# Up projection of a gated MLP: tokens as the stationary operand, gate and up columns side by side, and seven products for a part of it

## The chip, the core and the metric

The kernel runs on one core of a Trainium2 chip. A core has five engines with an instruction queue each: TensorE (PE, matrix products, its weight loads shown as PEld), VectorE (DVE), ScalarE (ACT), GpSimd (POOL) and SyncE (SP). TensorE reads operands from SBUF, the on-chip memory of 128 partitions, and writes to PSUM, which has eight banks of 128 x 512 float32. VectorE and ScalarE read and write both. DMA queues move data between HBM and SBUF; in this kernel SP issues the loads of weights.

The metric is the device time of one execution in microseconds. Before the change the runs shown took 1553.33, 1554.3 and 1554.38 us, median 1554.3.

## The reference

One layer of a decoder trunk over 256 tokens of width 2048: a token mixer (gated delta rule and pooling) with its input and output projections, then a gated MLP with a causal convolution, then a last norm. The change touches the MLP:

```python
        h = rmsnorm(x, norm_ffn_w[l])
        gate, up = jnp.split(jnp.einsum('bsd,df->bsf', h, w_up[l]), 2, axis=-1)
        gate = causal_dwconv(gate, conv_ffn_w[l]) + conv_ffn_b[l]
        x = x + jnp.einsum('bsf,fd->bsd', jax.nn.gelu(gate, approximate=False) * up, w_down[l])
    return rmsnorm(x, norm_final_w)
```

w_up is 2048 x 11264 (5632 columns of gate, then 5632 of up), w_down 5632 x 2048, the convolution reaches over three tokens. All is float32.

## The kernel before

**Products in three passes.** TensorE is given float32 data in a rounded form (F32R). Each operand is split into a high part and the remainder, and a product is the sum of high x high, low x high and high x low. A weight tile is 256 rows by 512 columns, held as 128 partitions x 2 x 512 ("raw", 512 KB). begin() (L198 to L219) loads it by SP, ScalarE casts it to whi (L209), VectorE subtracts to give wlo (L217). weights() (L145) hands out the next tile, in the order of the list srcs, and splits up to AHEAD = 2 tiles further on; whi and wlo have three buffers each, raw has four.

**Up projection (L1192 to L1221).** It goes over 11 pairs of 512 gate columns and 512 up columns; the list srcs (L95) holds for each pair first the eight gate tiles, then the eight up tiles. gemm_b() (L256) makes one of the two: the weight tile is the stationary operand, 128 columns at a time, and the tokens move, high and low part side by side as 512 columns (L272), then the high part alone against wlo as 256 columns (L273). So a tile takes eight couples of matmuls. The result lies in four banks with features on partitions and tokens along the free dimension, and it takes the banks of psm and psg in turn, so that one result can be emptied while the next is made. merged() (L277) adds the two halves of a bank; ScalarE and VectorE then scale by the norm (rb2, a row of factors copied over the partitions, L1165), convolve along tokens with one tensor_scalar and two scalar_tensor_tensor (L1200, L1204), apply Gelu (L1206), multiply by up (L1208) and split the product into hhi and hlo (L1215, L1216), the operands of the down projection.

**Down projection (L1256 on).** Here tokens are the stationary operand, and the 512 columns of a weight tile move. products() (L1244) issues for one tile and 128 tokens two times three matmuls of 512 columns; a plain tile is 12 matmuls. Three of the 11 feature chunks, SEVEN = (4, 9, 10), are made by Strassen's scheme in Winograd's form: a 2 x 2 block product (two halves of the tokens, two of the features, two of the columns) by seven products instead of eight, with sums of activations made by half_sums() (L1175) and sums of weights T1 to T4 made by VectorE in the buffer of the loaded block ("quad", quarter() at L161, the subtraction at L204). A product is six matmuls and has its own split weights. Between the products stand plain tiles.

**Turning.** turned() (L285) transposes a 256 x 512 block on TensorE, 16 transposes of 128 x 128 in two banks; before the change the mixer alone calls it (L293).

**Order.** From the output projection on, the order of the instructions on each engine's queue comes from a planner, which takes among those that it believes ready the one that stands first in the program; issue_after() puts the instructions of a block behind a given one on its engine. On the chip each queue runs strictly in that order.

**Names in the changed code.** xt holds the residual; fhl the normed tokens, high and low, features on partitions, in four tiles of 512 features (fhl[0] is features 0 to 511); rs2 is the norm's factor for each token. pm() gives two banks of the pool psm (two such buffers), pg() one bank of psg (four).

Of the kernel before, what the change touches and what calls it, by code (L numbers as in the profile page):

```python
# [14 lines left out]
P = 128  # L15
# [20 lines left out]
def kernel(  # L36
# [58 lines left out]
    for c in range(DFF // 512):  # L95
        srcs += cols(w_up[0], 512 * c, KD) + cols(w_up[0], DFF + 512 * c, KD)
    down = [cols(w_down[0], 512 * c, KF) for c in range(4)]

    SEVEN = (4, 9, 10)
# [59 lines left out]
    quarters = {}  # L159

    def quarter(half, chunk, what):  # L161

        if what == "11":
# [34 lines left out]
    def begin(n):  # L198
        while len(made) < min(len(srcs), n):
            load(len(made) + 1)  # L200
            raw = loads[len(made)]
            if isinstance(raw, tuple):
                raw, plus, minus = raw
                nc.vector.tensor_tensor(raw, plus, minus, op=ALU.subtract)  # L204
            shape = list(raw.shape)
# [13 lines left out]
            made.append((hi, lo))  # L219

# [912 lines left out]
    xt = fp.tile([P, 2, D], F32, name="xt")  # L1133
# [5 lines left out]
    for c in range(4):  # L1139
# [24 lines left out]
    rb2 = cpool.tile([P, S], F32, tag="rb", name="rb2")  # L1164
    rs2 = rstd_rows(ssq2, rb2)  # L1165
# [7 lines left out]
    def half_sums(c):  # L1173

        h = whole[c]  # L1175
        a11, a12, a21, a22 = (h[:, 2 * j : 2 * j + 2, t * P : (t + 1) * P] for t in range(2) for j in range(2))
        s = fp.tile([P, 4, S], F32, tag="y", name=nm("sums"))
# [5 lines left out]
        if c == SEVEN[1]:  # L1183
            hi, lo = (lambda b: (b[:, 0], b[:, 1]))(big.tile([P, 2, 4, S], F32R, tag="x3", name="sx"))
        else:
            more = dict(tag="gs", bufs=2) if c == SEVEN[2] else {}
            hi, lo = (fp.tile([P, 4, S], F32R, name=f"s{n}{c}", **more) for n in ("hi", "lo"))
        nc.scalar.copy(hi, s)
        nc.vector.tensor_tensor(lo, s, hi.bitcast(F32), op=ALU.subtract)
        sums_of[c] = (hi, lo)  # L1190

    rb2b = rb2.unsqueeze(1).to_broadcast([P, 4, S])  # L1192
    for c in range(DFF // 512):
        ps = gemm_b(lambda k: both(fhl, k), KD)
        gs = fp.tile([P, 4, S], F32, tag="gs", bufs=2, name=nm("gs"))
        nc.vector.tensor_tensor(gs, merged(ps, gs), rb2b, op=ALU.mult)
        y = fp.tile([P, 4, S], F32, tag="y", name=nm("y"))
        for f in range(4):
            r = 4 * c + f
            nc.vector.tensor_scalar(y[:, f, :], gs[:, f, :], cfw[:, 2 * KF + r : 2 * KF + r + 1],  # L1200
                                    vec[:, V_CB + r : V_CB + r + 1], op0=ALU.mult, op1=ALU.add)
            for j in (1, 0):
                s = 2 - j
                nc.vector.scalar_tensor_tensor(y[:, f, s:], gs[:, f, : S - s], cfw[:, j * KF + r : j * KF + r + 1],  # L1204
                                               y[:, f, s:], op0=ALU.mult, op1=ALU.add)
        nc.scalar.activation(y, y, AF.Gelu)  # L1206
        ps = gemm_b(lambda k: both(fhl, k), KD)
        nc.vector.tensor_tensor(gs, merged(ps, gs), y, op=ALU.mult)  # L1208
# [6 lines left out]
        nc.scalar.copy(hh, gs)  # L1215
        nc.vector.tensor_tensor(hl, gs, hh.bitcast(F32), op=ALU.subtract)  # L1216
        hhi.append(hh)
        hlo.append(hl)
        whole[c] = gs
        if c == SEVEN[0]:  # L1220
            half_sums(c)  # L1221
# [3 lines left out]
    lh, ll = at(hhi), at(hlo)  # L1225
# [17 lines left out]

    def products(ps, high, low, w, first, last, cs=slice(0, 512), shared=False):  # L1244
        for kk in range(2):
            for n, (part_, lhs) in enumerate(((w[0], high), (w[0], low), (w[1], high))):
                mm(ps[:, cs], lhs(kk), part_[:, kk, cs], start=(first and kk == 0 and n == 0),  # L1247
# [153 lines left out]
```

## Time and profile before

| what | value |
|---|---|
| median of three runs | 1554.3 us |
| profiled execution | 1552.15 us |
| its span, first to last instruction | 1550.4 us |
| granted TensorE clock, mean | 0.998 |
| read from HBM / written | 299.66 MB / 5.28 MB |

The busy time of an engine is a share of the span. A row of a group tells line, engine, operation, what it writes and reads, count, busy time, mean length of one in ns, and the engine's idle time ahead of it with what ended it. Timeline rows begin with the start in us and the length in us; a matmul's record is longer than the spacing between two matmuls, since they overlap. A row of stretches tells for each engine its busy time and, as (x...), how many instructions touch the stretch, then the granted clock, the DMA share and GB/s. Rows of one line of the kernel give minimum, median and maximum in ns, and the first and last start.

### The profile page before, as it was taken

What the parts mean: (1) busy time and instruction counts of PE and PEld (TensorE: products, weight loads), DVE (VectorE), ACT (ScalarE), POOL (GpSimd) and SP (SyncE); (2) the same over time, 40 slices, a digit from 0 to 9 for tenths busy, and PEclk for the clock granted to TensorE, in tenths of its full rate; (3) what the DMA queues carried; (4) which work ended last, traced back from release to release, by engine and by line L of the source; (5) the groups of instructions that cost most, each with busy time, mean ns of one, the idle gap of its engine ahead of it and who ended that gap; (6) DMA issues with size and microseconds to landing.
All of it is one profiled execution on the core that took longest, in us unless ns stands there. A gap on an engine that the chain in (4) does not pass through costs nothing.

```text
span 1550.4 us, 21200 instructions
## 1 busy us (share of the span) xinstructions
PE 1541.6 (99%) x7942; PEld 1294.1 (83%) x7942; DVE 1151.4 (74%) x1749; ACT 770.3 (50%) x987; POOL 39.3 (3%) x54
## 2 busy tenths in 40 slices
PE   9999999999999999999999999999999999999998
PEld 8888888788888888888888888888888888888886
DVE  6788858996689858886656667767666677877885
ACT  6445446454545446454554544444444444555552
POOL 1010001000100000000000000000000000000000
PEclk9999999999999999999999999999999999999999
DMA  8776757776576756675656666666666668557662
GB/s 274 214 219 206 204 152 223 215 209 183 170 237 202 208 164 202 217 206 175 215 181 185 187 186 188 189 190 189 184 195 186 187 189 271 176 190 231 201 209 93
DMA packets 165846, 306.34 MB, mean 198 GB/s; under 512 B 19138, under 2 KB 23010, under 8 KB 165614
## 3 DMA queue, kind: packets, MB, share of 16 engines
q1 hardware_dynamic: 162720, 299.95, 64.2%
q10 hardware_dynamic: 3022, 5.03, 1.0%
q8 instruction: 62, 1.02, 0.3%
q14 instruction: 42, 0.34, 0.1%
HBM read 299.66 MB, written 5.28 MB: 197 GB/s over the span
## 4 chain that ended last, share of the span: by engine, by line
PE 98%; issue 1%; DMA 1%; DVE 0%; ACT 0%; POOL 0%; POOLq 0%; ACTq 0%
PE psm L250 15%; PE psm L248 15%; PE psm L249 15%; PE psm L272 11%; PE psg L272 11%; PE psm L1247 7%; PE psg L1247 7%; PE psg L273 5%; PE psm L273 5%; PE psm L391 1%; PE psg L293 1%; PE psg L781 1%; PE psg L783 0%; DMA vrow<-ev 0%; PE psm L309 0%
## 5 line engine op out<-in xcount | busy, mean ns | idle before, releaser
L209 ACT CAST whi<-raw 128x1024 fp32r<-128x1024 f32 x500 | 526.0, 1052 | 612.9 <-PE psm L249 281.8
L217 DVE TENSOR_TENSOR wlo<-raw,whi 128x1024 fp32r<-128x1024 f32 x498 | 607.3, 1222 | 287.6 <-ACT whi L209 284.5
L250 PE MATMUL psm<-wlo,xhl 128*128 128x512 f32 x864 | 339.7, 393 | 0.6 <-DVE wlo L217 0.6
L248 PE MATMUL psm<-whi,xhl 128*128 128x512 f32 x864 | 338.6, 392 | 0.0
L249 PE MATMUL psm<-whi,xhl 128*128 128x512 f32 x864 | 337.9, 391 | 0.0
L272 PE MATMUL psm<-fhl,whi 128*128 128x512 f32 x704 | 246.1, 396 | 0.0
L272 PE MATMUL psg<-fhl,whi 128*128 128x512 f32 x704 | 238.2, 395 | 0.0
L273 PE MATMUL psm<-fhl,wlo 128*128 128x256 f32 x704 | 194.3, 279 | 0.0
L250 PEld LDWEIGHTS psm<-wlo,xhl 128*128 128x128 f32 x864 | 162.2, 188 | 35.1 <-DVE wlo L217 1.9
L249 PEld LDWEIGHTS psm<-whi,xhl 128*128 128x128 f32 x864 | 162.3, 188 | 33.4
L248 PEld LDWEIGHTS psm<-whi,xhl 128*128 128x128 f32 x864 | 162.3, 188 | 33.3 <-issue 0.2
L273 PE MATMUL psg<-fhl,wlo 128*128 128x256 f32 x704 | 178.9, 280 | 0.0
L272 PEld LDWEIGHTS psm<-fhl,whi 128*128 128x128 f32 x704 | 131.3, 188 | 30.4
L272 PEld LDWEIGHTS psg<-fhl,whi 128*128 128x128 f32 x704 | 129.2, 188 | 24.3
L273 PEld LDWEIGHTS psg<-fhl,wlo 128*128 128x128 f32 x704 | 132.5, 188 | 6.9
L273 PEld LDWEIGHTS psm<-fhl,wlo 128*128 128x128 f32 x704 | 132.6, 188 | 1.2
L209 ACT CAST whi<-quad 128x1024 fp32r<-128x1024 f32 x42 | 44.3, 1054 | 47.5 <-PE psm L1247 27.6
L217 DVE TENSOR_TENSOR wlo<-quad,whi 128x1024 fp32r<-128x1024 f32 x42 | 51.3, 1222 | 18.0 <-ACT whi L209 17.3
L1247 PE MATMUL psm<-whi,hhi 128*128 128x512 f32 (+1 forms) x150 | 58.0, 387 | 0.0
L1247 PE MATMUL psm<-whi,hlo 128*128 128x512 f32 (+1 forms) x150 | 58.0, 386 | 0.0
L1247 PE MATMUL psm<-wlo,hhi 128*128 128x512 f32 (+1 forms) x150 | 57.8, 386 | 0.0
L248 PE MATMUL psm<-whi,mhi 128*128 128x512 f32 x128 | 50.9, 397 | 0.0
(323 smaller groups left out, 1699.4 us busy)
## 6 DMA issues: line engine op xcount, KB each, us to landing
raw<-in_w_in_dram SPq DMA_DIRECT2D x224, 512.0 KB, 4.2
raw<-in_w_up_dram SPq DMA_DIRECT2D x176, 512.0 KB, 4.5
raw<-in_w_down_dram SPq DMA_DIRECT2D x64, 512.0 KB, 4.6
raw<-in_w_out_dram SPq DMA_DIRECT2D x32, 512.0 KB, 3.8
quad<-in_w_down_dram SPq DMA_DIRECT2D x12, 1024.0 KB, 6.2
mv<-vrow SPq DMA_DIRECT2D x12, 512.0 KB, 4.4
taps<-in_conv_qkv_w_dram SPq DMA_DIRECT2D x16, 256.0 KB, 6.5
raw<-in_pool_w_dram SPq DMA_DIRECT2D x8, 512.0 KB, 3.9
```

What stands on the lines that cost most here:

```text
L209: nc.scalar.copy(hi, raw)
L217: last_split[0] = nc.vector.tensor_tensor(lo, raw, hi.bitcast(F32), op=ALU.subtract).ins
L248: mm(ps[:, t, :], lh(k, t), hi[:, kk, :], start=(k == 0), stop=False)
L249: mm(ps[:, t, :], ll(k, t), hi[:, kk, :], start=False, stop=False)
L250: mm(ps[:, t, :], lh(k, t), lo[:, kk, :], start=False, stop=(k == nk - 1))
L272: mm(ps[f], hi[:, kk, fs], rhl(k), start=(k == 0), stop=False, skip_group_check=True)
L273: mm(ps[f][:, 1, :], lo[:, kk, fs], rhl(k)[:, 0, :], start=False, stop=(k == nk - 1), skip_group_check=True)
L293: nc.tensor.transpose(pt[:, ff, t * P : (t + 1) * P], src[:, t, f * P : (f + 1) * P], ident)
L391: mm(ps_k0[:, t, :], part(k, t), w[:, kk, :], start=(k == 0 and w is hi and part is xh), stop=(k == KD - 1 and w is lo))
L781: mm(pg0, kq[:, h, 0, 0:P], kq[:, h, :, :], start=True, stop=True)
L1247: mm(ps[:, cs], lhs(kk), part_[:, kk, cs], start=(first and kk == 0 and n == 0), stop=(last and kk == 1 and n == 2), skip_group_check=shared)
```

## The change

1. The order of the weight tiles in the up projection: gate and up tiles of a pair alternate (gate one ahead). Both results of a pair are made in four banks at once: (column, token half) with column 0 for gate and 1 for up.
2. Tokens are the stationary operand and the weight's 512 columns move, by products(), as in the down projection.
3. For pairs 1 to 10 the first 512 of the 2048 contracted features (FOUR = 0, four of the 16 tiles) are made by seven products. The 2 x 2 block is: token halves, the two halves of these features, and gate and up as the two halves of the columns. Sums of activations are made once (up_sums); sums of weights for each pair in a buffer "quad" of the tag xt. The banks of the pair serve as accumulators: product 11 is copied by ScalarE to another bank, two sums are written by VectorE into the others, and one bank carries the running sum. The seven stand ahead of the pair's 12 whole tiles.
4. The result has tokens on partitions. ScalarE copies it out of PSUM (gate scaled by rs2), TensorE turns it with turned(), in the midst of the next pair's seven products; ScalarE makes the first tap of the convolution, VectorE the two others, from PSUM. The last pair is turned at the head of the down projection.
5. The residual xt is stored to DRAM and loaded again after the up projection, since quad takes its place in SBUF.
6. In the down projection SEVEN becomes (8, 9, 10); the activations of chunks 8 and 9 are put together from their high and low parts before they are summed.

```diff
+    FOUR = 0
+    UP_PARTS = ("T1", "11", "T2", "21", "T3", "22", "T4")
+    up_w = [(cols(w_up[0], 512 * c, KD), cols(w_up[0], DFF + 512 * c, KD)) for c in range(NUP)]
+    up_steps = []
+    for c in range(NUP):
+        kps = [kp for kp in range(KD // 2) if c == 0 or kp // 2 != FOUR]
+        order = [(0, kps[0])]
+        for a, b in zip(kps[1:], kps):
+            order += [(0, a), (1, b)]
+        order.append((1, kps[-1]))
+        if c:
+            srcs += [("up", c, what) for what in UP_PARTS]
+        srcs += [up_w[c][col][kp] for col, kp in order]
+        up_steps.append(order)
...
-    SEVEN = (4, 9, 10)
+    SEVEN = (8, 9, 10)
...
+    UP_BUFFER = {"11": 0, "T1": 1, "T2": 1, "T3": 0, "21": 2, "22": 3, "T4": 1}
+    def quad_load(c, n):
+        if n == 0:
+            t = fp.tile([P, 4, 2, 512], F32, tag="xt", name=nm("quad"))
+            for i in range(4):
+                up_quarters[i] = t[:, i]
+        i = (1, 0, 3, 2)[n]
+        last_load[0] = nc.sync.dma_start(up_quarters[i], up_w[c][i % 2][2 * FOUR + i // 2]).ins
+    def up_sum(what):
+        b11, b12, b21, b22 = (up_quarters[i] for i in range(4))
+        for out_, plus_, minus_ in {"T1": [(b12, b12, b11)], "T2": [(b12, b22, b12)],
+                                    "T3": [(b11, b12, b11), (b12, b12, b21)]}[what]:
+            nc.vector.tensor_tensor(out_, plus_, minus_, op=ALU.subtract)
...
             made.append((hi, lo))
+            if following is not None:
+                up_sum(following)
+            if isinstance(src, tuple) and src[2] == "T4":
+                last_quad_split[0] = last_split[0]
...
+        nc.scalar.dma_start(xt_d[:, :, c * 512 : (c + 1) * 512], xs)
...
-    rs2 = rstd_rows(ssq2, rb2)
+    rs2 = rstd_rows(ssq2, None)
...
+    def gate_part(c, pts):
+        y = fp.tile([P, 4, S], F32, tag="y", name=nm("y"))
+        for f in range(4):
+            r = 4 * c + f
+            pt = pts[f // 2][:, f % 2, :]
+            with tc.issue_after(last_copy[0]) if c < NUP - 1 else ExitStack():
+                nc.scalar.activation(y[:, f, :], pt, AF.Identity, scale=cfw[:, 2 * KF + r : 2 * KF + r + 1],
+                                     bias=vec[:, V_CB + r : V_CB + r + 1])
+            with tc.issue_after(last_quad_split[0]) if c < NUP - 1 else ExitStack():
+                for j in (1, 0):
+                    s = 2 - j
+                    nc.vector.scalar_tensor_tensor(y[:, f, s:], pt[:, : S - s], cfw[:, j * KF + r : j * KF + r + 1],
+                                                   y[:, f, s:], op0=ALU.mult, op1=ALU.add)
+            if f == 1:
+                yield
         nc.scalar.activation(y, y, AF.Gelu)
...
+    def up_part(c, pts):
+        y = whole[c]
+        for f2, pt in enumerate(pts):
+            fs = slice(2 * f2, 2 * f2 + 2)
+            nc.vector.tensor_tensor(y[:, fs], pt, y[:, fs], op=ALU.mult)
...
+    def split_parts(c):
+        ups = up_ups[0]
+        bank = banks_of[c]
+        y = pg()
...
+        chain_ = bank[0, 1]
+        part("T1", y, True)
+        own = cpool.tile([P, 512], F32, tag="sqj", name=nm("own"))
+        nc.scalar.copy(own, y)
+        part("11", chain_, True)
+        last_copy[0] = nc.scalar.copy(bank[0, 0], chain_).ins
+        yield
+        part("T2", chain_, False)
+        nc.vector.tensor_tensor(bank[1, 0], chain_, own, op=ALU.add)
+        part("21", bank[0, 0], False)
+        yield
+        part("T3", chain_, False)
+        nc.vector.tensor_tensor(bank[1, 1], chain_, own, op=ALU.add)
+        part("22", bank[1, 0], False)
+        part("T4", chain_, False)
...
+    for c in range(NUP):
+        pair = [pm(), pm()]
+        banks_of[c] = {(0, 0): pair[0][:, 0], (1, 0): pair[0][:, 1], (1, 1): pair[1][:, 0], (0, 1): pair[1][:, 1]}
+        bank = banks_of[c]
+        if c:
+            parts = split_parts(c)
+            next(parts)
+            gates = gate_part(c - 1, turned(pending[0]))
+            next(parts)
+            ups = turned(pending[1])
+            for _ in parts:
+                pass
+        steps_ = up_steps[c]
+        left = len(steps_)
+        pending = []
+        for n, (col, kp) in enumerate(steps_):
+            left -= 1
+            w = weights()
+            for t in range(2):
+                products(bank[col, t], lambda kk: fh(2 * kp + kk, t), lambda kk: fl(2 * kp + kk, t), w,
+                         c == 0 and kp == 0, not any(q[0] == col for q in steps_[n + 1 :]), shared=True)
+            if c and n < 3:
+                next(gates) if n < 2 else up_part(c - 1, ups)
+            if c + 1 < NUP:
+                if left in (8, 7, 6, 5):
+                    quad_load(c + 1, 8 - left)
+                if left == 4:
+                    up_sum("T1")
+            if not any(q[0] == col for q in steps_[n + 1 :]):
+                e = fp.tile([P, 2, 512], F32, tag=("eg", "eu")[col], name=nm("e"))
+                for t in (0, 1) if col == 0 else (1, 0):
+                    if col == 0:
+                        nc.scalar.activation(e[:, t, :], bank[col, t], AF.Copy, scale=rs2[:, t : t + 1])
+                    else:
+                        nc.scalar.copy(e[:, t, :], bank[col, t])
+                pending.append(e)
+            if c == 0 and n == 8:
+                up_ups.append(up_sums())
+            if c == NUP - 1 and n == 5:
+                half_sums(SEVEN[0])
+    xt = fp.tile([P, 2, D], F32, tag="xt", name="xt")
+    for c in range(4):
+        nc.scalar.dma_start(xt[:, :, c * 512 : (c + 1) * 512], xt_d[:, :, c * 512 : (c + 1) * 512])
...
+            if hf == 0 and n == 1:
+                for _ in gate_part(NUP - 1, turned(pending[0])):
+                    pass
+            if hf == 0 and n == 2:
+                up_part(NUP - 1, turned(pending[1]))
```

In the code a product is named by the weights it takes: 11, 21 and 22 are loaded tiles, T1 to T4 sums of them. eg and eu are the copies of the gate and up banks in SBUF.

More of the change, by code (lines that the diff above doesn't have):

```diff
@@ L204, in begin @@
                 nc.vector.tensor_tensor(raw, plus, minus, op=ALU.subtract)
+            src = srcs[len(made)]
+            following = {"T1": "T2", "T2": "T3"}.get(src[2]) if isinstance(src, tuple) and src[0] == "up" else None
             shape = list(raw.shape)
@@ L1171, with four_sums @@
     sums_of = {}
[L1173 to L1177, printed above, removed]
+    def four_sums(a11, a12, a21, a22, hi, lo):
+        s = fp.tile([P, 4, S], F32, tag="s", name=nm("sums"))
         s1, s2, s3, s4 = (s[:, n].rearrange("p (k s) -> p k s", k=2) for n in range(4))
@@ L1242, in weighted @@
         nc.vector.tensor_tensor(block(t, c), block(t, c), nfin[:, c * 512 : (c + 1) * 512], op=ALU.mult)
[L1244 to L1247, printed above, removed]
-                   stop=(last and kk == 1 and n == 2), skip_group_check=shared)
     def direct(ps, kp, t, w, first, last, **more):
```

89 lines of the change are left out of this document (59 added, 30 removed).

## The prediction

> **What bounds the kernel now.** Read first: the page's head, its busy times, and the chain that ended last by engine.
>
> ```profile
> span 1550.4 us, 21200 instructions
> PE 1541.6 (99%) x7942; PEld 1294.1 (83%) x7942; DVE 1151.4 (74%) x1749; ACT 770.3 (50%) x987; POOL 39.3 (3%) x54
> PE 98%; issue 1%; DMA 1%; DVE 0%; ACT 0%; POOL 0%; POOLq 0%; ACTq 0%
> ```
>
> TensorE is on the path for 98% of the span, so a change is worth the spacing of its matmuls less whatever makes TensorE wait. Next the up projection: the timeline at its two edges, the chain of waits where one place recurs in each pair of gate and up columns, and busy time by stretch.
>
> ```profile
> 817.72 0.39 PE L272 MATMUL psm<-fhl,whi 128*128 128x512 f32 x1
> 1311.26 0.40 PE L1247 MATMUL psm<-whi,hhi 128*128 128x512 f32 x1
> ...
> 897.70 0.69 PE psg L272 x3
> 1121.42 0.69 PE psg L272 x3
> ...
> 932.00:977.00 45.00, 45.00 (x259) 39.26 (x259) 30.04 (x39) 21.73 (x28) 0.00 (x0) 1.00 0.64 188
> 1350.00:1450.00 100.00, 100.00 (x443) 82.81 (x442) 78.31 (x75) 51.68 (x56) 0.00 (x0) 1.00 0.58 188
> ```
>
> The stage runs from 817.72 to 1311.26, 493.5 us. Between 897.70 and 1121.42 lie five pairs: 44.74 us each, 2.796 for each of a pair's 16 weight tiles, 0.3496 for each two matmuls (512 and 256 columns) of L272 and L273. In the 45 us stretch TensorE never stops, VectorE works 30.0 us and ScalarE 21.7. The last row is the down projection, whose matmuls already have tokens as the stationary operand and 512 columns: 443 touch the 100 us, about two of them only at the edges, so one starts every 100/441 = 0.227 us.
>
> **The change part by part.** *Matmul form.* A weight tile goes from eight couples (8 x 0.3496 = 2.796) to twelve matmuls of 512 columns (12 x 0.227 = 2.722). The number of columns is the same; what is saved is what a couple takes beyond its columns. [...]
>
> *Seven products.* In ten of eleven pairs four of the 16 tiles (48 matmuls) become seven products of six. Tiles used whole: 16 + 10 x 12 = 136, so 136 x 12 + 10 x 42 = 2052 matmuls, 2052 x 0.2268 = 465.4 us.
>
> *Turning.* Each pair's result is turned by 16 transposes, which fall on TensorE, those of the last pair in the down projection. The same helper is in the trace, as the chain shows it:
>
> ```profile
> 241.09 1.75 PE psg L293 x16
> 758.51 0.87 PE psg L293 x8
> ...
> L293 PE MATMUL psg<-ident,sz x32: 270/272/273, 240.9 to 759.1; 128*128 128x128 f32 x32
> ```
>
> Eight cost 0.875 us of the path, though each record is 272 ns long: they overlap. Eleven pairs: 22 x 0.875 = 19.3 us. [...]
>
> *Sum of TensorE's own work.* Before 493.5. After 465.4 + 19.3, and 0.9 for the eight transposes of L1154 that stand in both: 485.6. Gone too are the two small matmuls for rb2, 0.3 at most, within the rounding. So -8.0 us, if TensorE waits no more than now. Without the seven products it would be 13.6 us worse (60 matmuls), so their cost decides.
>
> *The stretch of seven products.* They come one after another at the head of each pair, a product lasting 6 x 0.227 = 1.36 us where a whole tile lasts 2.72, and only two tiles are split ahead (three buffers). Each product needs a cast on ScalarE and a subtraction on VectorE, and between them VectorE makes T2, T3 and T4 and adds two banks. Durations:
>
> ```profile
> L209 ACT CAST whi<-quad 128x1024 fp32r<-128x1024 f32 x42 | 44.3, 1054 | 47.5 <-PE psm L1247 27.6
> L217 DVE TENSOR_TENSOR wlo<-quad,whi 128x1024 fp32r<-128x1024 f32 x42 | 51.3, 1222 | 18.0 <-ACT whi L209 17.3
> ...
> 1319.91 1.22 DVE L204 TENSOR_TENSOR quad<-quad 128x1024 f32<-128x1024 f32 x1
> 1321.05 1.22 DVE L217 TENSOR_TENSOR wlo<-quad,whi 128x1024 fp32r<-128x1024 f32 x1
> 1322.18 1.22 DVE L1189 TENSOR_TENSOR sx<-sums,sx 128x1024 fp32r<-128x1024 f32 x1
> ...
> L1296 ACT COPY u<-psg x1: 572/572/572, 1387.1 to 1387.1; 128x512 f32<-128x512 f32 x1
> L1298 DVE TENSOR_TENSOR u<-u,psg x1: 681/681/681, 1404.7 to 1404.7; 128x512 f32<-128x512 f32 x1
> ```
>
> Back to back, VectorE starts one of 1024 elements every 1.135 us. Let 0 be the first matmul of T1; T1 and 11 are split by then, since tiles before them last 2.72 each. T2 must wait for the buffer of the pair's last whole tile. What ScalarE does first at that moment is seen in the present kernel at such an edge:
>
> ```profile
> 1310.91 0.40 PE L272 MATMUL psg<-fhl,whi 128*128 128x512 f32 x1
> 1311.14 0.28 PE L273 MATMUL psg<-fhl,wlo 128*128 128x256 f32 x1
> 1311.34 1.05 ACT L209 CAST whi<-raw 128x1024 fp32r<-128x1024 f32 x1 [0.21 <-PE psg L272]
> 1312.30 0.36 ACT L281 COPY lh<-psg 128x256 f32<-128x256 f32 x1
> ```
>
> The cast starts when the last matmul that reads whi ends (1311.31), one matmul before the bank is complete (1311.42), so it goes ahead of the copy that empties the bank. I take the same here: T2's cast 0 to 1.05, then the up bank's copy to 1.6, until when product 11 waits about 0.3 (that copy frees the pair of banks its chain is in). From 1.07 VectorE has T2's subtraction, T3 and T4, the subtractions of 21 and T3, an add, those of 22 and T4, and an add: seven of 1.135 and two of 0.64 to 0.68 (those by L1298; the operand in SBUF and the result in PSUM are the other way round, a loss or gain of a tenth is all I allow). The second add ends at 1.07 + 7.95 + 1.32 = 10.34, and product T4 writes the bank that it read. How TensorE restarts after such a wait:
>
> ```profile
> 280.81 1.22 DVE L217 TENSOR_TENSOR wlo<-raw,whi 128x1024 fp32r<-128x1024 f32 x1
> 282.08 0.50 PE L250 MATMUL psm<-wlo,xhl 128*128 128x512 f32 x1 [0.32 <-DVE wlo L217]
> 282.43 0.40 PE L248 MATMUL psm<-whi,xhl 128*128 128x512 f32 x1
> ```
>
> 0.05 after VectorE's end, and 0.35 to the next matmul in place of 0.23. So T4 ends near 10.34 + 0.05 + 0.12 + 1.36 = 11.87, where work alone (42 x 0.227 + 1.75) ends at 11.28: 0.6 late. TensorE's own order gives nearly the same: 0.3 for product 11, hidden thereafter since ScalarE's copy of 11 (0.57, behind 21's cast) lies under eight transposes and the first add under product 21 and eight more. I take 0.55 a pair, 5.5 us in ten. Bounds: nothing, if all fits in the slack (TensorE's 11.28 against VectorE's 9.3 of work); 1.4, if the two copies of the up banks go ahead of T2's cast on ScalarE (0.8 later for all that follows).
>
> *What is moved off.* Emptying the banks (four copies of 0.57, two before the pair ends), the first tap on ScalarE, the two other taps on VectorE out of PSUM, and the product with up lie under the twelve whole tiles, 32.7 us. There VectorE has twelve splits, T1's sum, eight taps, two products and hlo:
>
> ```profile
> L1204 DVE SCALAR_TENSOR_TENSOR y<-gs,cfw,y 128x255 f32<-128x255 f32 x32 | 14.0, 478 | 0.0
> ```
>
> 14 x 1.22 + 8 x 0.48 + 2 x 0.68 = 22.3 of 32.7 us. The order that holds the taps behind T4's split keeps them out of the stretch before. Over a pair VectorE works about 36 us of 44.6, up from 30: nothing by itself; without that order 3.8 us of taps would fall on the stretch.
>
> *DMAs.* Bytes of weights are unchanged; four of the 16 tiles come through one buffer, issued on SP's queue between the raw loads once the previous pair's T4 is split, some 10 us before T1's sum wants the first two.
>
> ```profile
> raw<-in_w_up_dram SPq DMA_DIRECT2D x176, 512.0 KB, 4.5
> xt<-in_x_dram ACTq DMA_DIRECT2D x4, 512.0 KB, 8.1
> nfin<-in_norm_final_w_dram ACTq DMA_DIRECT2D x1, 1024.0 KB, 6.2
> ```
>
> A load takes 4.5 us, so no wait. The residual goes out in four stores and comes back in four loads on ScalarE's queue, ahead of nfin; behind a waiting one stand ScalarE's casts, but the buffer is free after the last pair's T4, long before. Their 4 MB lie beside 188 GB/s of other traffic and are wanted 90 us later: nothing.
>
> *Head of the down projection.* The last pair's taps move here, and chunk 9 is put together anew for its sums (chunk 8 before the edge).
>
> ```profile
> 1311.00:1350.00 39.00, 39.00 (x174) 32.15 (x173) 33.85 (x38) 22.35 (x23) 0.00 (x0) 1.00 0.61 209
> ```
>
> VectorE has 5 us free in these 39 and gets about 3.8 + 1.4 + 1.2 - 2.0 = 4.4 more. Two tiles split ahead cover most of it: 0.5, bounds 0 and 2.
>
> The sum: -8.0 + 5.5 + 0.5 = -2.0. The profiled execution took 1552.15 (span 1550.4 and 1.75 around it); it would take 1550.15. The median of the runs, 1554.3, lies 2.15 above it: 1552.3.
>
> **The rivals.** *Slower: ScalarE's order at the head of a pair.* If the bank copies stand ahead of T2's cast, VectorE starts 0.8 later and each pair loses about 1.4: -8.0 + 14 + 0.5 = +6.5, 1560.8. For it: both are due within 0.15 us; against: the four rows at 1311. It decides against the change from 0.75 a pair on.
> *VectorE as the bound of the stretch.* If on top of that order its nine instructions don't follow each other closely, each waiting about 0.1 for a cast or a release, because TensorE and VectorE alternate: 1.4 + 0.9 = 2.3 a pair: +15.5, 1570. Against: the closely packed rows at 1319.91.
> *Everything hidden.* If T2's cast and the chain of adds cost TensorE nothing: -8.0, 1546.3. For it: VectorE's 9.3 us are less than 11.28; against: only two tiles are split ahead, so the 1.05 of T2's cast can't be spread.
>
> **How the numbers follow.** A measurement tells about 0.2%, 3.1 us, from no change. The forecast (waits of 0.2 to 0.9 a pair) has 0.50, its own range 1549 to 1556; all hidden 0.13; ScalarE's order 0.27; VectorE's bound 0.10. Faster by over 0.2% (below 1551.2): the hidden case and half of the forecast's span, 0.39. Within: 0.21. Slower (above 1557.4): the two slow cases and the forecast's upper tail, 0.40. The range reaches from the hidden case to above the slower rival: 1546 to 1566; what VectorE's bound would add is left out.
>
> **What would show it.** A whole tile every 2.72 us and eight transposes in 0.87 confirm -8.0 of work. A pair of 44.5 us from T1 to T1 confirms the forecast; 43.97 is all hidden; 45.4 is ScalarE's order, to be seen as bank copies ahead of T2's cast. Waits of TensorE should stand on the adds and on wlo of T2, 21 and T4 alone. Waits inside the whole tiles, on a DMA, or of over 2 us after 1311 would make the prediction wrong.

## The result and the profile after

The changed kernel took 1579.41 us (median of 4 runs, 1576.23 to 1580.13) against 1553.82 for the kernel before on the same chip: ratio 1.0163, interval 1.0145 to 1.018. It is slower by 25.6 us, where 2.0 less were forecast, and the time lies above the range.

The page of the changed kernel, its head, its busy times and its chain that ended last by engine:

```profile
span 1577.5 us, 20038 instructions
PE 1550.1 (98%) x7350; PEld 1264.2 (80%) x7350; DVE 1188.9 (75%) x1712; ACT 826.1 (52%) x1038; POOL 45.1 (3%) x54
PE 89%; DVE 5%; DMA 2%; ACT 2%; issue 2%; POOL 0%; POOLq 0%; ACTq 0%; DVEq 0%
```

TensorE's busy share is nearly as high as before (98 against 99%), and tells nothing: its records, 0.39 us long at starts 0.227 apart, overlap, and a matmul counts as busy while it runs on. The chain tells: TensorE's share fell from 98 to 89%, and VectorE, DMA and ScalarE, which had 1% together, now have 9%. TensorE waits for others.

Where, by the timeline of the changed kernel (start, length): the first matmul of the up stage, T1 of a pair in its middle and of one late in it, the first matmul of the down projection.

```profile
817.41 0.39 PE L1289 MATMUL psm<-whi,fhl 128*128 128x512 f32 x1
951.96 0.63 PE L1289 MATMUL psg<-whi,ups 128*128 128x512 f32 x2
1229.82 0.39 PE L1289 MATMUL psg<-whi,ups 128*128 128x512 f32 x1
1333.17 0.47 PE L1289 MATMUL psm<-whi,hhi 128*128 128x512 f32 x1
```

The stage takes 1333.17 - 817.41 = 515.8 us, 22.2 more than before. Between 951.96 and 1229.82 lie six pairs: 46.31 each. The trace of the stage has 2052 matmuls and 176 transposes, as counted in the prediction; at 0.2268 and 0.109 they are 465.4 + 19.2 = 484.6 us of work. So 31.1 us are waits, which the kernel before did not have here. A pair holds 186 matmuls and 16 transposes from T1 to T1, 43.93 of work; 2.37 are lost in each of nine such stretches (21.4 in all), 9.5 in the last pair, which ends in the down projection, and 0.2 ahead of the first T1. From the first down matmul to the end it is 244.3 against 239.2, 5.1 more. Work 484.6 - 493.5 = -8.9, waits +31.1, the end +5.1, and a start 0.3 earlier: +27.0, and the spans differ by 27.1.

**A pair.** The same kernel's waits over the stage (engine and line, what it waited for, us in total, times, longest), those of TensorE with most time:

```profile
PEld psm L1289 <- DVE psm L1322: 14.0, 10, 2.3
PE psm L1289 <- DVE psm L1322: 9.7, 10, 1.9
PEld psm L1289 <- ACT whi L244: 9.4, 12, 2.6
PEld psm L1289 <- ACT e L1366: 3.3, 11, 0.4
```

L1322 is the first of VectorE's two adds, which writes the bank of the second column (up) and the first token half, (1, 0). It occurs ten times, once in each pair with seven products. Around it in one pair, from the timeline:

```profile
954.00 1.05 ACT L244 CAST whi<-quad 128x1024 fp32r<-128x1024 f32 x1 [1.26 <-PE psm L1289]
955.09 1.23 DVE L252 TENSOR_TENSOR wlo<-quad,whi 128x1024 fp32r<-128x1024 f32 x1 [2.48 <-ACT whi L244]
...
960.62 0.40 PE L1289 MATMUL psm<-wlo,ups 128*128 128x512 f32 x1
...
961.13 0.70 DVE L1322 TENSOR_TENSOR psm<-psm,own 128x512 f32<-128x512 f32 x1
...
961.88 0.73 PE L1289 MATMUL psm<-whi,fhl 128*128 128x512 f32 x2 [0.86 <-DVE psm L1322]
...
965.60 0.87 DVE L1261 SCALAR_TENSOR_TENSOR y<-psg,cfw,y 128x255 f32<-128x255 f32 x2
...
966.39 0.69 DVE L1326 TENSOR_TENSOR psm<-psm,own 128x512 f32<-128x512 f32 x1
```

At 960.62 starts the last matmul of T2, at 961.88 the first of product 21: 1.26 apart where 0.227 is the rhythm. Product 21 writes the bank (0, 0). The add between them writes (1, 0): another bank, but the other half of the same two-bank buffer, pair[0]. That product has no use for the add's result. Also, two taps stand on VectorE's queue at 965.60, ahead of the second add (L1326), for which T4 has to wait. And the cast of product 11's weights starts only at 954.00, 2.0 us after T1 began; VectorE stands idle for 2.48 us ahead of 955.09, at the start of its chain. Of the pair's 2.37, the gaps between starts give 1.03 + 0.11 (a restart takes 0.34 in place of 0.23) at product 21 and 0.7 at the second add; the other 0.5 are small restarts.

**The last pair.** Two adds are late here, and a load, as the timeline shows:

```profile
1285.21 1.22 DVE L1235 TENSOR_TENSOR whole<-hhi,hlo 128x1024 f32<-128x1024 f32 x1
1286.35 0.69 DVE L1322 TENSOR_TENSOR psm<-psm,own 128x512 f32<-128x512 f32 x1
1287.10 0.73 PE L1289 MATMUL psm<-whi,fhl 128*128 128x512 f32 x2 [1.91 <-DVE psm L1322]
...
1291.47 0.59 ACTq L1377 DMA_DIRECT2D xt<-xtd  x1
...
1306.82 1.04 ACT L244 CAST whi<-raw 128x1024 fp32r<-128x1024 f32 x1 [8.33 <-DMA raw<-in_w_up_dram]
...
1307.91 1.21 PE L1289 MATMUL psm<-whi,fhl 128*128 128x512 f32 x4 [2.13 <-ACT whi L244]
```

Chunk 8 is put together on VectorE (L1235) just ahead of the first add, and its sums ahead of T4's split: TensorE waits 2.08 at 1284.8 and 1.93 at 1291.1 beyond its rhythm. Then a tile's cast waits 8.33 us for its load. The loads issued from 1288 to 1310, with KB each and the median us from issue to landing:

```profile
raw<-in_w_up_dram SPq DMA_DIRECT2D x5, 512.0 KB, 10.6
xt<-xtd ACTq DMA_DIRECT2D x4, 512.0 KB, 9.3
nfin<-in_norm_final_w_dram ACTq DMA_DIRECT2D x1, 1024.0 KB
```

The residual (2 MB read) and the last norm's weights (1 MB) come at once with weights that have no lead; a weight tile takes 10.6 us in place of the page's 4.7. TensorE waits 2.29 beyond its rhythm, and its next 14 matmuls come 0.23 to 0.62 apart instead of 0.227 (some 2.3 more); the granted clock was 0.50 from 1309.8 to 1313.2.

**The down projection.** Two waits of TensorE, from the timeline:

```profile
1350.60 0.50 PE L1289 MATMUL psm<-wlo,hhi 128*128 128x512 f32 x1 [1.64 <-DVE wlo L252]
...
1491.11 1.04 ACT L244 CAST khi<-raw 128x1024 fp32r<-128x1024 f32 x1 [2.59 <-DMA raw<-in_w_down_dram]
...
1493.15 0.50 PE L1289 MATMUL psg<-whi,hhi 128*128 128x512 f32 x1 [1.68 <-ACT whi L244]
```

At the head VectorE is full with taps, sums and splits: 1.8 beyond the rhythm. At 1491 a cast that TensorE needs stands on ScalarE behind that of a tile kept for the end (khi), which waits for its load: 1.85. With eight transposes (0.9) and restarts these make the 5.1.

### The profile page after: what moved, and what is told of

The parts are those of the page before. It is cut to its first block, busy times and chain, and to the rows that moved or that the text cites. A ratio compares the mean times of both kernels' runs of the same rounds, so it can differ in the third digit from the quotient of the medians.

```text
span 1577.5 us, 20038 instructions
## 1 busy us (share of the span) xinstructions
PE 1550.1 (98%) x7350; PEld 1264.2 (80%) x7350; DVE 1188.9 (75%) x1712; ACT 826.1 (52%) x1038; POOL 45.1 (3%) x54
## 4 chain that ended last, share of the span: by engine, by line
PE 89%; DVE 5%; DMA 2%; ACT 2%; issue 2%; POOL 0%; POOLq 0%; ACTq 0%; DVEq 0%
PE psm L1289 32%; PE psm L289 15%; PE psm L287 15%; PE psm L288 14%; PE psg L1289 7%; DVE wlo L252 2%; ACT whi L244 2%; PE psm L430 1%; DVE quad L190 1%; PE psg L332 1%; PE psg L820 1%; DMA raw<-in_w_up_dram 1%; DVE psm L1322 0%; DMA raw<-in_w_down_dram 0%; DVE psm L1326 0%
## 5 line engine op out<-in xcount | busy, mean ns | idle before, releaser
L252 DVE TENSOR_TENSOR wlo<-raw,whi 128x1024 fp32r<-128x1024 f32 x458 | 557.2, 1221 | 223.7 <-ACT whi L244 221.1
L1289 PE MATMUL psm<-whi,fhl 128*128 128x512 f32 x1208 | 363.7, 396 | 14.9 <-DVE psm L1322 9.7
L1289 PEld LDWEIGHTS psm<-whi,fhl 128*128 128x128 f32 x1208 | 222.4, 188 | 75.0 <-DVE psm L1322 14.0
L1289 PE MATMUL psm<-wlo,fhl 128*128 128x512 f32 x604 | 218.1, 391 | 0.0
L252 DVE TENSOR_TENSOR wlo<-quad,whi 128x1024 fp32r<-128x1024 f32 x112 | 136.0, 1222 | 62.6 <-ACT whi L244 62.2
L244 ACT CAST whi<-quad 128x1024 fp32r<-128x1024 f32 x112 | 116.8, 1053 | 77.9 <-PE psm L1289 55.2
L1289 PEld LDWEIGHTS psm<-wlo,fhl 128*128 128x128 f32 x604 | 113.7, 188 | 25.0 <-DVE wlo L252 0.8
L1289 PE MATMUL psg<-whi,hhi 128*128 128x512 f32 (+1 forms) x130 | 50.3, 387 | 1.7 <-ACT whi L244 1.7
L1289 PE MATMUL psg<-whi,hlo 128*128 128x512 f32 (+1 forms) x130 | 50.2, 386 | 0.0
L289 PE MATMUL psm<-wlo,mhi 128*128 128x512 f32 x128 | 50.0, 390 | 0.0
```

What stands on the lines that cost most here:

```text
L244: nc.scalar.copy(hi, raw)
L252: last_split[0] = nc.vector.tensor_tensor(lo, raw, hi.bitcast(F32), op=ALU.subtract).ins
L289: mm(ps[:, t, :], lh(k, t), lo[:, kk, :], start=False, stop=(k == nk - 1))
```

## The experiments

The theory after this reading: the program orders TensorE's write to one bank of a two-bank buffer behind other engines' access to the other bank; what is left is the order on ScalarE's and VectorE's queues. The rival: VectorE has too much to do in the stretch of seven products.

**swap_banks**: the four banks are paired otherwise.

```diff
-        banks_of[c] = {(0, 0): pair[0][:, 0], (1, 0): pair[0][:, 1], (1, 1): pair[1][:, 0], (0, 1): pair[1][:, 1]}
+        banks_of[c] = {(0, 0): pair[0][:, 0], (1, 1): pair[0][:, 1], (1, 0): pair[1][:, 0], (0, 1): pair[1][:, 1]}
```

> Edit: the pairing of banks in the two psm buffers alone; gate of the first tokens and up of the second share a buffer, up of the first and gate of the second the other. Theory A (a matmul into one bank of a buffer is made to wait for VectorE's or ScalarE's access to the other bank): product 21 no longer waits for the first add (1.03 us and 0.11 of restart a pair); a pair falls from 46.31 to 45.1 to 45.6, the span from 1577.5 to 1566 to 1571. Theory B (VectorE's chain of nine instructions is the bound of the stretch of seven products): 21 starts sooner, T4 waits as much longer; a pair stays at 46.1 to 46.4, the span within 2 us.

Measured: 1592.28 us, ratio 1.0253 (1.0232 to 1.0273), a pair 47.6 to 48.2, the first 49.1. Both numbers missed. The timeline of this kernel:

```profile
966.34 0.69 DVE L1322 TENSOR_TENSOR psm<-psm,own 128x512 f32<-128x512 f32 x1
966.94 3.48 DVE L252 TENSOR_TENSOR wlo<-quad,whi 128x1024 fp32r<-128x1024 f32 x3
...
971.13 0.69 DVE L1326 TENSOR_TENSOR psm<-psm,own 128x512 f32<-128x512 f32 x1
...
971.96 0.70 PE L1289 MATMUL psm<-whi,ups 128*128 128x512 f32 x2 [2.55 <-DVE psm L1326]
```

The wait on the first add is gone, as the theory had it. In its place product 22, which writes (1, 0), waits 2.95 us from start to start for the second add, which reads (0, 1), now the other half of its buffer; and that add stands on VectorE behind three splits (966.94, 3.48) and taps. A wait that only the pairing decides moves when the pairing does; what it costs depends on what stands ahead of the add.

**single_banks**: from the up projection on, four buffers of one bank each in place of two of two banks.

```diff
+    def two():
+        return [ps1.tile([P, 512], F32, tag="m1", name=nm("ps1")) for _ in range(2)]
...
-        pair = [pm(), pm()]
-        banks_of[c] = {(0, 0): pair[0][:, 0], (1, 0): pair[0][:, 1], (1, 1): pair[1][:, 0], (0, 1): pair[1][:, 1]}
+        pair = [two(), two()]
+        banks_of[c] = {(0, 0): pair[0][0], (1, 0): pair[0][1], (1, 1): pair[1][0], (0, 1): pair[1][1]}
```

> Edit: from the up projection on, four buffers of one bank each in place of two buffers of two; nothing else. Theory A: besides 21's wait, the last two whole tiles no longer wait for the copy of the gate bank in the same buffer, so they run in their order, T1's and 11's casts come sooner and VectorE's chain starts about 1.5 us sooner; a pair falls to 44.3 to 44.9 (work alone is 43.97), the span by 14 to 20 us to 1558 to 1564. Theory B: a pair stays above 46, the span above 1574.

Measured: 1570.96 us, ratio 1.0116 (1.01 to 1.0133), a pair 45.57 in the mean: better by 0.74, which lies between the two theories. The timeline, in which T1 starts at 956.38:

```profile
954.72 1.23 DVE L254 TENSOR_TENSOR wlo<-quad,whi 128x1024 fp32r<-128x1024 f32 x1 [0.24 <-ACT whi L246]
...
957.48 1.22 DVE L254 TENSOR_TENSOR wlo<-quad,whi 128x1024 fp32r<-128x1024 f32 x1 [0.28 <-ACT whi L246]
...
960.07 1.05 ACT L246 CAST whi<-quad 128x1024 fp32r<-128x1024 f32 x1 [0.41 <-ACT own L1325]
...
961.02 0.58 ACT L1327 COPY ps<-ps 128x512 f32<-128x512 f32 x1
...
961.65 0.73 PE L1297 MATMUL ps<-whi,ups 128*128 128x512 f32 x2 [0.57 <-ACT ps L1327]
...
963.15 0.62 PE L1297 MATMUL ps<-whi,fhl 128*128 128x512 f32 x2
963.35 0.70 DVE L1330 TENSOR_TENSOR ps<-ps,own 128x512 f32<-128x512 f32 x1 [0.98 <-PE ps L1297]
...
966.72 0.87 DVE L1269 SCALAR_TENSOR_TENSOR y<-psg,cfw,y 128x255 f32<-128x255 f32 x2
...
967.50 0.69 DVE L1334 TENSOR_TENSOR ps<-ps,own 128x512 f32<-128x512 f32 x1
...
968.25 0.73 PE L1297 MATMUL ps<-whi,fhl 128*128 128x512 f32 x2 [0.40 <-DVE ps L1334]
```

The lines at 963.15 and 963.35 show the lock gone: product 21 starts in rhythm, ahead of the first add, and its matmuls go on at 963.61 and 963.83 while the add runs on another bank, from 963.35 to 964.05. So the wait of 1.03 us came from the program, which makes a write wait for the whole buffer. The first two rows are the subtractions for products 11 and T2: 11's is now done ahead of T1, and T2's starts 1.1 us after T1, where in the changed kernel they start 3.1 and 4.5 us after it (955.09 and 956.50 against 951.96). What is left are two real needs that are served late. T2 adds to the bank that ScalarE's copy of product 11 reads, and that copy (961.02) stands behind a cast (960.07) that is wanted later: 0.61 + 0.11. T4 waits for the second add (967.50), which stands behind taps (966.72) that are wanted much later: 0.56 + 0.11. The stage also starts 4 us later (821.61 against 817.41), as the buffers are changed just ahead of it.

**no_sums**: the three subtractions that make T2, T3 and T4 are left out, so these products take the buffers as they are. (In the changed kernel T4 is b21 - b12; the diff under The change has the two operands exchanged.)

```diff
-            nc.vector.tensor_tensor(out_, plus_, minus_, op=ALU.subtract)
+            if what == "T1":
+                nc.vector.tensor_tensor(out_, plus_, minus_, op=ALU.subtract)
```

> Leaves out the three subtractions on VectorE that make T2, T3 and T4 from the loaded blocks (T1's stays), so products T2, T3 and T4 take other numbers; TensorE's and ScalarE's work is the same. VectorE has 3 x 1.14 = 3.4 us a pair less in the stretch. Theory A: the first add starts only when T2 is through on TensorE, so 21's wait for it stays at about 1 us; a pair 45.6 to 46.2, span -1 to -7. Theory B: all of the 2.3 us of waits go; a pair 43.9 to 44.3, span -20.

Measured: 1584.67 us (one run), a pair 46.95, outside both. This speaks against the rival: with three sums of 1.22 us less on VectorE in each stretch a pair did not become shorter but 0.6 longer. The order on the queues shifted with it, so by itself it doesn't settle the matter; ordered, below, does. The timeline:

```profile
964.64 0.70 DVE L1323 TENSOR_TENSOR psm<-psm,own 128x512 f32<-128x512 f32 x1 [1.04 <-PE psm L1290]
...
965.39 0.73 PE L1290 MATMUL psm<-whi,fhl 128*128 128x512 f32 x2 [0.86 <-DVE psm L1323]
```

VectorE was idle for 1.04 us ahead of the add, waiting for TensorE, and TensorE still waited 0.86 for the add. At this place it is a delay that TensorE and VectorE pass to each other, not a queue that is too long.

**no_seven**: all 16 tiles whole in every pair, no products; tokens stationary and turning as in the change.

```diff
-        kps = [kp for kp in range(KD // 2) if c == 0 or kp // 2 != FOUR]
+        kps = list(range(KD // 2))
...
-        if c:
-            srcs += [("up", c, what) for what in UP_PARTS]
```

> Edit: all 16 tiles of each pair are taken whole, no seven products, no sums of weights or activations for them; tokens stationary, alternating columns, turning, stores of the residual and the down projection as in the changed kernel. TensorE's work by the prediction: a whole tile 12 x 0.227 = 2.72, 8 transposes 0.875; a pair 43.6 + 1.75 = 45.3, the up stage's work 13.6 us above that of the changed kernel. Theory A: little wait is left, since nothing is added within a pair; only the last tiles wait for the gate bank's copy (0.2 a pair): a pair 45.3 to 45.6, span 1568 to 1572 if the waits after the last pair (8.6 and 3.8 us) stay, 1556 to 1560 if they go with the seven products. Theory B: the same pair.

Measured: 1564.84 us, ratio 1.0075 (1.006 to 1.009), a pair 45.55 as expected, span 1561.9, between the two ranges and nearer to the one in which the waits after the last pair go. The edges of the stage:

```profile
817.88 0.39 PE L1287 MATMUL psm<-whi,fhl 128*128 128x512 f32 x1
1318.89 0.48 PE L1287 MATMUL psm<-whi,hhi 128*128 128x512 f32 x1
```

501.0 us, with 498.3 of work (2112 matmuls, 176 transposes) and only 2.8 of waits. So the new form without the products is 7.5 slower than the old stage, and the products, which save 60 matmuls in all (13.6 us), bring 31.1 - 2.8 = 28.3 of waits, those of the last pair among them. The seven are where the change is lost.

**reload_late**: the residual is loaded again behind a cast in the down projection's 15th step, not at the end of the up stage.

```diff
+            if hf == 0 and n == 14:
+                with tc.issue_after(last_cast[0]):
+                    xt = fp.tile([P, 2, D], F32, tag="xt", name="xt")
+                    for c in range(4):
+                        nc.scalar.dma_start(xt[:, :, c * 512 : (c + 1) * 512], xt_d[:, :, c * 512 : (c + 1) * 512])
```

> Edit on the changed kernel: the four loads that bring the residual back stand behind a cast at the fifteenth step of the down projection instead of ahead of the last pair's whole tiles; nothing else. Theory C (in the last pair 2 MB of residual and 1 MB of nfin compete with the weight tiles that TensorE wants at once): the waits at 1305 to 1314 (2.3 for a tile, 2.3 of half clock behind it) go, those on VectorE at 1285 and 1291 stay (2.6 more than in other pairs); span -4 to -6, 1571.5 to 1573.5; pairs stay at 46.31. If the tiles are late for another reason (their buffers come free late, after the seven products), the span stays within 1.5.

Measured: 1576.8 us, ratio 1.0152 (1.0132 to 1.0172); the span is 2.6 shorter, where 4 to 6 were expected. The wait at 1305 and the slow matmuls behind it are gone (4.6 us), so the reload made them. Part came back in the down projection and the end, which take 1.2 longer (0.6 at 1376 and 0.3 at 1519 among it), and this execution reached the stage 1.1 later. The two waits on VectorE in the last pair stayed, and a pair stayed at 46.31.

**ordered**: single banks (taken up from the second pair on, so that the stage starts as before), the copy of product 11 ahead of T3's cast on ScalarE, and the taps behind the second add on VectorE.

```diff
-        part("T2", chain_, False)
+        with tc.issue_after(last_copy[0]):
+            part("T2", chain_, False)
...
-        nc.vector.tensor_tensor(bank[1, 1], chain_, own, op=ALU.add)
+        last_add[0] = nc.vector.tensor_tensor(bank[1, 1], chain_, own, op=ALU.add).ins
...
-            with tc.issue_after(last_quad_split[0]) if c < NUP - 1 else ExitStack():
+            with tc.issue_after(last_add[0]) if c < NUP - 1 else ExitStack():
```

> Edit: single_banks, but with the change of buffers after the first pair, and two orders: on ScalarE product T3's cast stands behind the copy of 11 to the other bank; on VectorE the taps stand behind the second add, not behind T4's split. Theory A' (with the buffer lock gone, what is left of waits in single_banks, 0.72 before T2 and 0.67 before T4 a pair, is the order on the two queues, not their load): a pair falls from 45.57 to 44.1 to 44.4; with 3 to 4 us less at the start of the stage the span is 1569.7 - 12.5 - 3.5 = 1553.7, 1551 to 1557. Theory B' (load): a pair stays above 45.2, the span above 1563.

Measured: 1557.61 us, ratio 1.003 (1.0017 to 1.0043), span 1553.7, as the first theory has it. T1 of the two pairs as above, in this kernel:

```profile
951.71 0.63 PE L1291 MATMUL psg<-whi,ups 128*128 128x512 f32 x2
1217.46 0.39 PE L1291 MATMUL psg<-whi,ups 128*128 128x512 f32 x1
```

Six pairs in 265.75: 44.29 each, 0.36 above the work and no wait over 0.11 among it. One bank to a buffer and two orders, with not one instruction less, give back 2.0 of the 2.37 a pair, 0.74 by the banks (single_banks) and 1.28 by the orders. VectorE kept all its work, so its load is not what bounds the stretch.

**mended**: ordered, with the late reload and the sums of chunk 8 behind the last pair's second add.

```diff
             if c == NUP - 1 and n == 5:
-                half_sums(SEVEN[0])
+                with tc.issue_after(last_add[0]):
+                    half_sums(SEVEN[0])
```

> Edit: ordered, and the residual loaded again late as in reload_late, and chunk 8's sums behind the last pair's second add. Theory C: the last pair's extra waits (1.3 on VectorE, 3.3 on tiles in single_banks) go: span 4 to 5 us below ordered, about 1549, 1546 to 1553, which would be level with the kernel before or up to 4 us below it. Otherwise within 1.5 us of ordered.

Measured: 1555.9 us, ratio 1.0018 (1.0009 to 1.0028); the span fell by 1.0 only (the median by 1.7), where 4 to 5 were expected. The up stage is 489.1, 4.4 less than before the change and 2.6 less than in ordered, but the down projection and the end take 246.1, against 239.2 before the change and 244.3 in ordered. The timeline of this kernel:

```profile
1339.11 2.61 ACTq L1437 DMA_DIRECT2D xt<-xtd  x4
...
1354.02 1.05 ACT L247 CAST whi<-quad 128x1024 fp32r<-128x1024 f32 x1 [6.15 <-DMA quad<-in_w_down_dram]
...
1355.12 0.50 PE L1292 MATMUL ps<-whi,hhi 128*128 128x512 f32 x1 [1.32 <-ACT whi L247]
```

The late reload meets the load of a product's block, whose cast waits 6.15 us. The reload is not free there either.

Three more, together: **sums_behind** is ordered with the diff of mended alone and the reload where the change has it; **spread_reload** puts each of its four loads behind a cast in the last pair, and the last norm's weights late; **late_keeps** adds a shift of the kept tiles.

```diff
+            if c == NUP - 1 and left in (8, 7, 6, 5):
+                if left == 8:
+                    xt = fp.tile([P, 2, D], F32, tag="xt", name="xt")
+                with tc.issue_after(last_cast[0]):
+                    i = 8 - left
+                    nc.scalar.dma_start(xt[:, :, i * 512 : (i + 1) * 512], xt_d[:, :, i * 512 : (i + 1) * 512])
...
-    stream(1, DIRECT[:-2], (3, 1, 1), (9, 13, 17, 21))
+    stream(1, DIRECT[:-2], (3, 1, 1), (11, 15, 19, 23))
```

> The kernel of the run ordered, with one thing more: the sums of chunk 8 stand behind the last pair's second add on VectorE; the residual is loaded again where the change put it. In ordered TensorE waits 1.4 us at 1285.5 and 0.3 at 1288 for splits that these sums put off, and nothing on a DMA near 1300. Theory (in ordered the reload costs nothing any more, only the order on VectorE does): both waits go, span 1551.5 to 1552.2, and the wait of 2.1 us at 1353 that the run mended had on a block's load is absent. Rival (the reload still costs, since the waits of the last pair only hid it): the waits come back on a DMA between 1300 and 1315, span 1553 to 1555.

> As sums_behind, with the four loads of the residual behind four casts on ScalarE's queue in the last pair, at the places where other pairs load a quarter of their block, and the load of the last norm's weights in the down projection's 21st step. Theory (what matters is that a load does not meet others that are due): no wait on a DMA between 1280 and 1360, span 1551 to 1552. Rival (the four loads, 4 MB read and written beside the weights, slow the weights wherever they stand): a wait of 1 to 2 us on raw or quad, span above 1552.5.

> As spread_reload, with the four weight tiles that are kept split for the end taken two plain tiles later in the second half of the down projection. In ordered and mended TensorE waits 1.2 to 1.6 us at 1467: the cast of a product's weights stands on ScalarE behind a kept tile's cast, which waits 2.4 us for its load. Theory (the place of the kept tile against the blocks' loads decides): that wait goes, span 1 to 1.5 us below that of spread_reload, 1549.5 to 1551, level with the kernel before (1550.4) or just below it. Rival (SP's queue is that far behind in any order there): the wait turns up at another tile and the span stays within 0.4.

The runs of one of these kernels lie 3 to 6 us apart, and the profiled one can be any of them: for ordered it was the fastest of five, for sums_behind and late_keeps the slowest. So spans 1 us apart rank nothing here; the medians and the single waits are what can be read.

sums_behind: 1557.27 us, ratio 1.0027 (1.0017 to 1.0038), span 1557.3, outside both. The wait of 1.3 at 1286 stayed although the sums had moved, so it was not theirs; the loads of weights in that stretch take 7.7 us to land, which speaks for the reload, as the rival has it. The wait behind a kept tile's cast at 1468, 1.40 beyond the rhythm in ordered, was 2.65 here, with slow matmuls behind it (last section).

spread_reload: 1556.66 us, ratio 1.0023 (1.0014 to 1.0032), span 1552.8. The wait at 1286 is gone and one of 0.75 stands at 1301: the rival's side, with a smaller number. Spreading lowers what the reload costs and does not remove it.

late_keeps: 1554.14 us, ratio 1.0009 (1.0 to 1.0018), in the median 2.5 below spread_reload. The wait at 1467 is gone, as the theory has it, for one of 1.0 at 1498. The profiled execution, span 1554.0, misses the number; it reached the up stage 2.2 later than that of spread_reload (820.21 against 818.03); from there to the end it takes 733.8 against 734.7. Its edges of the stage:

```profile
820.21 0.39 PE L1292 MATMUL psm<-whi,fhl 128*128 128x512 f32 x1
...
1310.60 0.39 PE L1292 MATMUL ps<-whi,hhi 128*128 128x512 f32 x1
```

490.4 against 493.5: the change's form of the stage is 3.1 ahead, and the down projection, with the last pair's turning and taps, the reload and the other place of the sums, takes 243.4 against 239.2. No version here beats the kernel before; this one is level with it.

## Why the prediction was wrong

*TensorE's own work* was right: 2052 matmuls and the transposes at the forecast durations, -8.9 in the stage and 0.9 of it back in the down projection, together the -8.0 of the sum (its own terms give -7.9).

*The stretch of seven products* is the step that failed: "I take 0.55 a pair, 5.5 us in ten", with bounds of 0 and 1.4. A pair lost 2.37, and the last pair 9.5, of which 4.6 are the reload's (below) and most of the rest stands at its two adds, behind the work for chunk 8, which the sum had not priced there: 31 us in the place of 5.5. The step followed each engine's work and the data that a product needs. It left out that a write to a bank also waits for whatever the program does with the other half of its buffer: 1.03 + 0.11 at product 21, shown by single_banks, where the wait went. The diff had the pairing of the banks; the step asked it once, for product 11 ("that copy frees the pair of banks its chain is in"), and not for the adds. The pairing also broke the step's first line, "T1 and 11 are split by then": twelve matmuls of whole tiles still ran behind T1's first two (952.56 to 955.17), so 11's cast had to wait for a buffer until 954.00, and T2's subtraction, the head of the step's chain, started 4.5 after T1 instead of the 1.07 of the step. In single_banks it started 1.1 after T1; how much of the 2.37 this makes by itself was not measured.

*The order on the queues* was the other part, 1.28 a pair by ordered against 0.74 by the banks alone. The step had the nine VectorE instructions one behind the other in the order of need; on the chip taps stood ahead of the second add and, once the banks were single, a cast ahead of the copy of 11. ordered put these right and a pair came to 44.29, 0.36 above the work and inside the forecast's waits of 0.2 to 0.9. So the forecast described a kernel whose orders are as the step assumed, and that was not the kernel at hand.

*The rivals.* VectorE as the bound gave 2.3 a pair, the measured size, by another mechanism: no_sums took part of its load away and the loss stayed, and ordered left it all its load and the loss went. The size was a coincidence. ScalarE's order named the right engine and the wrong instruction, and its 1.4 a pair was too small.

*DMAs: "nothing"* was wrong. The reload makes TensorE lose 4.6 us where the change has it, and 2.6 came off the span when it was moved (reload_late), since 2 MB, with the 1 MB of the last norm's weights, fall at once on a stretch in which weights are loaded just in time, and a weight tile took 10.6 us there in place of 4.7; the average of 188 GB/s said nothing of that stretch. Moved, it met another load (mended). That it is wanted 90 us later says when it must land, not what it pushes aside.

*The head of the down projection*, 0.5 with a bound of 2, took 1.8, inside the bound. The wait at 1491 was not in the sum: the new set of chunks, (8, 9, 10), or the later start shifts the kept tile's cast against its load; late_keeps shows that the place of the kept tiles decides, and no run separated what moved it.

Of the signs that it named against itself, a wait on a DMA came (at 1305), and waits of over 2 us after 1311 just about (2.03 at 1348 and 2.07 at 1491, from start to start); the sign that mattered, a pair of 44.5, failed by 1.8.

## What to carry over

When a change lets several engines touch accumulators in turn, write down for each write what else the program does in the same buffer, not only in the same bank (1.03 + 0.11 us a pair here), and what stands ahead of it on the other engine's queue: here one bank to a buffer and two orders brought the loss from 25.6 us down to 4.2, by the medians. A stage in which one engine hands results to another within 1.4 us must be costed by its chain (release, 0.7 of add, restart), since shares of busy time of 75 and 52% say that there is room and not that the work comes in time. A transfer is priced at the traffic of the stretch where it starts, and moving it asks the same question again at the new place: the reload cost TensorE 4.6 us at the first, and a cast waited 6.15 us at the second.

## What the hardware showed

TensorE's granted clock fell after one wait and not after another of the same length. Waits below are from start to start. In swap_banks a wait of 2.95 us came in nine pairs. After the first, at 872.1, the granted clock was 0.50 for 3.41 us; after a later one, at 969.0, it was 1.00. By stretches (busy time by engine, then the granted clock, the DMA share and GB/s):

```profile
871.35:874.77 3.42, 1.18 (x4) 0.65 (x4) 3.42 (x5) 1.28 (x2) 0.00 (x0) 1.00 0.08 4
874.77:878.18 3.41, 3.10 (x7) 2.48 (x8) 2.55 (x5) 1.11 (x2) 0.00 (x0) 0.50 0.93 330
878.18:881.60 3.42, 3.42 (x16) 2.82 (x15) 2.93 (x4) 2.02 (x3) 0.00 (x0) 1.00 1.05 393
...
966.93:970.34 3.41, 2.27 (x9) 1.24 (x7) 3.41 (x4) 2.47 (x3) 0.00 (x0) 1.00 0.00 0
970.34:973.75 3.41, 1.79 (x8) 1.53 (x9) 3.38 (x7) 0.36 (x1) 0.00 (x0) 1.00 0.64 185
```

The second row is the fall, from 874.77 to 878.18: 7 matmuls touch it, and 16 the row after it. In the row ahead of it TensorE was busy for 1.18 of 3.42 us; the wait at 969.0 is divided between the last two rows, where it was busy for 2.27 and 1.79 of 3.41. The changed kernel had the clock at 0.50 from 1309.8 to 1313.2, behind a wait of 2.52 us at 1305.4, and sums_behind at 0.57 in the mean from 1472 to 1476, behind one of 2.88 us at 1468.7. So the length of a wait did not tell whether the clock fell behind it; what did, no run separated.

Leaving out three sums in no_sums made a pair longer by 0.6 us, by the order on a queue: T3's cast, which no longer waits for a sum, goes ahead of ScalarE's copy of product 11 (961.29 and 962.24 in one pair, where the changed kernel has the copy at 958.73 and the cast at 960.13), and T2 waits 0.67 for that copy. Why the planner puts it first stays open.
